# Sums of weights on VectorE, a quarter of the first modulations on VectorE with constant matmuls in TensorE's wait, positions added twice

## The chip, the cores and the metric

The kernel runs on one core of a Trainium2 chip. The core has a matrix engine (TensorE, PE in the profile; PEld is its weight load), a vector engine (VectorE, DVE), an activation engine (ScalarE, ACT), a general engine (GpSimd, POOL) and a queue from which nearly all DMA transfers are issued (SyncE, SP). Each engine executes its own instructions in order and waits on semaphores for the others. The metric is the time of one execution on the device, in microseconds (us).

## The reference

One layer over 1024 latent tokens with 256 context tokens in front, width 1024, all in float32:

```python
h = x + grid_pos_emb(rows)[None]                      # fixed sin/cos of row and column
mods   = split(silu(c) @ w_ada + b_ada, 9)            # shift, scale, gate of three sublayers
mods_c = split(silu(c_ctx) @ w_ada + b_ada, 9)        # the same for the context
def ffn_sublayer(h, shift, scale, gate, g, w_in, w_out):
    hn = modulate(rmsnorm(h, g), shift, scale)        # x * (1 + scale) + shift
    a, b = split(hn @ w_in, 2)                        # 1024 -> 2 x 2816
    return h + 0.5 * gate * ((silu(a) * b) @ w_out)
h  = ffn_sublayer(h,  ..., w_ffn1_in, w_ffn1_out);  hc = ffn_sublayer(hc, ...)
p_lat = project(h, ..., w_in); p_ctx = project(hc, ...)   # q, k, v, gates, o, u, vs, ga, gb
# mLSTM in both directions, the context gives its first state; spatial gating MLP;
# both projected by w_a, w_b, merged by sigmoid gates, projected by w_o
h = h + mods[5] * merge_branches(...)
h = ffn_sublayer(h, ..., w_ffn2_in, w_ffn2_out)
return rmsnorm(h, g_final)
```

## The kernel before, in words

Activations lie with the feature dimension on the partitions: `h[tb][d]` is a tile of 128 features by 512 tokens (`tb` 0 or 1, `d` 0 to 7). Every large product is made to float32's accuracy from two reduced-precision halves: `split` (L142 to 144) makes the high half by a copy on ScalarE (L143) and the low half by a subtraction on DVE (L144), and `mm3` issues three matmuls per term. So each weight tile passes through ScalarE and DVE before PE may use it, and DVE's `ring`, `wring` and `hl` subtractions are what most matmuls wait for if anything.

The stages in order of time: the start (0 to 51 us), the context's FFN input product (to 178), the latent FFN's input product, called the first gate stage here (178 to 602), its output product `w1o` (602 to 812), the context's output product and the projections, the mLSTM and the merge (812 to 2021), the second gate stage (2021 to 2451), the second output product with the final norm (2451 to the end).

**The start.** The first two modulations need `silu(c) @ w_ada`. Four quarters `qt` of 256 features each are loaded as eight pages (`ada_pages`, 256 KB a page); for each page PE does a matmul (`ada_mm`, tile `adr`, L811, executed in two passes); `ada_out` brings the row onto the partitions by small matmuls (tile `adc`, L820), adds the bias into `mods` (L824) and makes `smod` (L831). Meanwhile the context is normed (`nct`): squares on ScalarE, their sum `acc` on DVE (L196), a sum over partitions on PE (`p`), rstd on DVE in eleven small steps, a diagonal (`diag`, L210) that PE turns into a broadcast (`rb`, L214). `mod0(d)` then makes the context page `hnc[d]`: `nt` on DVE (L225), the high half on ScalarE, the low half on POOL for even `d` (L229), on DVE for odd `d` (L232). With `hnc` and split weights (`W.load`: tiles `raw` and `hl`) PE runs `proj` (`pa` and `pb`, L169). Ten matmuls on a constant (`junk`) fill PE before the first page.

**The gate stages.** Their class makes blocks of the product from seven smaller ones instead of eight, so sums and differences of weight blocks are needed: `presum` (L355, L356), the block of product 6 (L371) and of product 3 (L373), all on POOL (`G`), ahead of the split. A weight tile loaded for that is `rawq` (`rawh` for the first tiles of a stage). The class `Rows` does the like for the matrices of the mixing part (L1140 to L1146).

**w1o.** The class for it runs seven products in the order 1, 2, 4, 7, 6, 5, 3, of eleven steps each. A step loads a page of activations (`graw` or `gring`), for the first two products a weight page (`rw`), splits them and runs its matmuls. After product 2 the results are added to `h`, which `res` (L664) loads back from the spill buffer `hsp`; the start had stored h plus positions there.

**Order.** The program emits work in one order; a scheduler places each engine's instructions. `slow`, `later` and `todo` are queues of small functions; `pump` takes one from them as matmuls give credit (512 for three matmuls of 512 columns), and each function has a cost. So vector work is spread between matmuls at a rate that the costs set.

## Time and profile before

| | |
|---|---|
| median of 3 runs | 2685.7 us (2684.61 to 2685.88) |
| the profiled execution's own time | 2682.41 us |
| its span, first to last instruction | 2680.3 us |
| mean granted PE clock | 0.997 |
| PE busy | 2650.2 us (99%) |
| DVE busy | 1916.7 us (72%) |
| ACT busy | 1141.7 us (43%) |
| POOL busy | 440.6 us (16%) |
| DMA | 456.73 MB, mean 170 GB/s |

A row of the timeline or of a group names line, engine, operation and the tiles it writes and reads; a bracket at the end of a timeline row gives the idle time before it and whose end it waited for. Rows with an A.BC:D.EF stretch give each engine's busy time in that stretch, the granted clock (1.00 is full), the DMA share and GB/s. `x16` counts instructions as executed.

### The profile page before, as it was taken

What the parts mean: (1) busy time and instruction counts of PE and PEld (TensorE: products, weight loads), DVE (VectorE), ACT (ScalarE), POOL (GpSimd) and SP (SyncE); (2) the same over time, 40 slices, a digit from 0 to 9 for tenths busy, and PEclk for the clock granted to TensorE, in tenths of its full rate; (3) what the DMA queues carried; (4) which work ended last, traced back from release to release, by engine and by line L of the source; (5) the groups of instructions that cost most, each with busy time, mean ns of one, the idle gap of its engine ahead of it and who ended that gap; (6) DMA issues with size and microseconds to landing.
All of it is one profiled execution on the core that took longest, in us unless ns stands there. A gap on an engine that the chain in (4) does not pass through costs nothing.

```text
span 2680.3 us, 35678 instructions
## 1 busy us (share of the span) xinstructions
PE 2650.2 (99%) x12754; PEld 2210.3 (82%) x12754; DVE 1916.7 (72%) x3243; ACT 1141.7 (43%) x1952; POOL 440.6 (16%) x422
## 2 busy tenths in 40 slices
PE   9999999999999999999999999999999999999998
PEld 5998888888889878888888888888887788888887
DVE  4897688686979646687664868677568766675855
ACT  4664444344336525564443443121245444344432
POOL 0041333220000210000002005342102323230000
PEclk9999999999999999999999999999999999999999
DMA  8842344369578222356553467448140332337645
GB/s 299 315 173 99 142 165 149 114 217 327 156 254 281 85 79 86 106 169 199 194 176 105 140 238 268 166 167 279 58 159 24 126 140 99 135 122 274 201 157 173
DMA packets 202240, 456.73 MB, mean 170 GB/s; under 512 B 20432, under 2 KB 54480, under 8 KB 202064
## 3 DMA queue, kind: packets, MB, share of 16 engines
q1 hardware_dynamic: 202064, 454.47, 49.6%
q8 instruction: 100, 1.64, 0.3%
q14 instruction: 76, 0.62, 0.1%
HBM read 328.95 MB, written 125.51 MB: 170 GB/s over the span
## 4 chain that ended last, share of the span: by engine, by line
PE 89%; DVE 6%; issue 2%; DMA 1%; ACT 1%; SPq 0%; POOL 0%; POOLq 0%; ACTq 0%; DVEq 0%
PE pq L1240 17%; PE qa L389 17%; PE po L508 14%; PE qb L389 12%; PE pt L1719 9%; PE pr L1159 6%; PE pc L1030 2%; PE pn L1832 2%; PE pu L1559 2%; PE pa L169 1%; PE pb L169 1%; PE pkc L1219 1%; PE adr L811 1%; PE pn L1830 1%; DVE h L292 1%
## 5 line engine op out<-in xcount | busy, mean ns | idle before, releaser
L144 DVE TENSOR_TENSOR ring<-rawq,ring 128x512 fp32r<-128x512 f32 x408 | 310.6, 762 | 204.9 <-ACT ring L143 202.2
L508 PE MATMUL po<-gring,wring 128*128 128x512 f32 (+1 forms) x1896 | 425.1, 385 | 0.5 <-DMA gring<-fsp 0.5
L508 PEld LDWEIGHTS po<-gring,wring 128*128 128x128 f32 x1896 | 349.5, 188 | 71.9 <-issue 1.0
L143 ACT CAST ring<-rawq 128x512 fp32r<-128x512 f32 x408 | 252.9, 621 | 299.5 <-PE pq L1240 82.1
L389 PE MATMUL qa<-fc,ring 128*128 128x512 f32 x1056 | 252.6, 390 | 2.3 <-DVE ring L144 1.4
L389 PEld LDWEIGHTS qa<-fc,ring 128*128 128x128 f32 x1056 | 198.1, 188 | 44.2 <-DVE ring L144 1.8
L1240 PE MATMUL pq<-fc,ring 128*128 128x512 f32 x864 | 207.8, 393 | 0.0
L143 ACT CAST wring<-rw 128x512 fp32r<-128x512 f32 x154 | 95.9, 622 | 228.3 <-PE po L508 220.9
L1240 PEld LDWEIGHTS pq<-fc,ring 128*128 128x128 f32 x864 | 161.6, 188 | 33.3
L1719 PE MATMUL pt<-yp,ring 128*128 128x512 f32 x768 | 183.9, 396 | 1.2 <-ACT ug L1297 1.2
L144 DVE TENSOR_TENSOR wring<-rw,wring 128x512 fp32r<-128x512 f32 x154 | 106.3, 691 | 93.9 <-ACT wring L143 93.7
L1719 PEld LDWEIGHTS pt<-yp,ring 128*128 128x128 f32 x768 | 144.2, 188 | 30.7 <-ACT ug L1297 1.4
L1240 PE MATMUL pq<-fa,ring 128*128 128x512 f32 x576 | 142.3, 395 | 0.0
L1240 PE MATMUL pq<-fb,ring 128*128 128x512 f32 x576 | 138.2, 394 | 0.0
L389 PE MATMUL qa<-fb,ring 128*128 128x512 f32 x528 | 128.6, 394 | 3.7 <-ACT p L404 3.7
L389 PE MATMUL qa<-fa,ring 128*128 128x512 f32 x528 | 127.7, 391 | 1.2 <-DVE ring L144 0.7
L389 PE MATMUL qb<-fb,ring 128*128 128x512 f32 x528 | 126.8, 390 | 1.2 <-DVE p L406 0.6
L1240 PEld LDWEIGHTS pq<-fb,ring 128*128 128x128 f32 x576 | 107.7, 188 | 23.7 <-issue 0.2
L389 PE MATMUL qb<-fa,ring 128*128 128x512 f32 x528 | 126.2, 389 | 0.0
L389 PE MATMUL qb<-fc,ring 128*128 128x512 f32 x528 | 126.2, 389 | 0.0
L751 DVE SCALAR_TENSOR_TENSOR adacc<-adapg,sc,adacc 128x512 f32<-128x512 f32 x140 | 111.4, 814 | 20.1 <-DMA adapg<-in_w_ada_dram 19.3
L1240 PEld LDWEIGHTS pq<-fa,ring 128*128 128x128 f32 x576 | 106.9, 188 | 22.5 <-DVE ring L144 0.2
(342 smaller groups left out, 4803.9 us busy)
## 6 DMA issues: line engine op xcount, KB each, us to landing
adapg<-in_w_ada_dram SPq DMA_DIRECT2D x144, 256.0 KB, 3.7
fsp<-fhl SPq DMA_DIRECT2D x66, 512.0 KB, 2.6
gring<-fsp SPq DMA_DIRECT2D x66, 512.0 KB, 4.2
raw<-in_w1i_dram SPq DMA_DIRECT2D x44, 512.0 KB, 5.5
graw<-fsp SPq DMA_DIRECT2D x88, 256.0 KB, 3.6
rawq<-in_w1i_dram SPq DMA_DIRECT2D x38, 512.0 KB, 3.4
rawq<-in_w2i_dram SPq DMA_DIRECT2D x38, 512.0 KB, 3.6
fsp<-p SPq DMA_DIRECT2D x66, 256.0 KB, 2.1
```

What stands on the lines that cost most here:

```text
L143: S.copy(hl[:, 0, :], src)
L144: V.tensor_sub(hl[:, 1, :], src, hl[:, 0, :].bitcast(F32))
L169: T.matmul(pt, x, y, start=first and i == 0, stop=i == n - 1, skip_group_check=True)
L389: T.matmul(pt, hl[:, x, sl], pages[p][k][:, y, :], start=first and i == 0, stop=i == 11, skip_group_check=not first)
L508: T.matmul(pt[:, cs], w[:, x, sl], g[:, y, cs], start=grp and kp == 0 and i == 0, stop=kp == NFP - 1 and i == 2, skip_group_check=not grp)
L751: eng.scalar_tensor_tensor(acc, pgt, sc2[:, q, k:k + 1], acc, ALU.mult, ALU.add)
L1030: T.matmul(pt, hl[d // 4][:, x, sl], g[:, y, :], start=f == 0 and d % 2 == 0 and i == 0, stop=f == NF - 1 and i == 2, skip_group_check=True)
L1159: T.matmul(self.pt[m], pg[:, x, sl], hl[:, y, :], start=first and k == 0 and i == 0, stop=k == 3 and i == 2, skip_group_check=not first)
L1240: T.matmul(pt, hl[:, x, k * 128:(k + 1) * 128], pg[k][:, y, :], start=first and k == 0 and i == 0, stop=k == 3 and i == 2, skip_group_chec ...
L1559: T.matmul(pu[:, 0:257], ksl[:, kt * 128:(kt + 1) * 128], wv, start=True, stop=True)
L1719: T.matmul(pt, hl[:, x, k * 128:(k + 1) * 128], pg[:, y, :], start=kh + k + i == 0, stop=kh == 1 and k == 3 and i == 2)
L1832: T.matmul(pn[:, 0:257], qi[:, c_, :], self.C[d][:, c_, :], start=False, stop=c_ == 1)
```

## The change

1. At the start, quarter 3 is no longer multiplied on PE. Its pages are accumulated on DVE, page times `silu(c)` for the two conditions, then transposed and reduced, and summed over partition groups by one matmul per condition on the constant `grp4` (new function `ada_side`). The pages of quarter 1 and quarter 3 are loaded alternately, then quarter 2; seven more `junk` matmuls stand behind quarter 0; quarter 1's matmuls are cut in two around the sum of squares; the context pages are used in the order 0 to 3, 6, 7, 4, 5; `pos` and most constants are loaded later.
2. h plus positions isn't stored at the start. In w1o x is loaded again from the input during the second product, and the positions are added a second time (function `base`, tile `pos2`, 16 DVE additions).
3. The sums of weights of the gate stages and of the row matrices run on DVE instead of POOL; the sums of the first stage's first six tiles stay on POOL (`A.preload(G)`).
4. Small moves: the gap ahead of the context's second norm pages, two more empty steps before the second gate stage's broadcast, pages of `yp` and `raw` taken from the other half of a pool, x loaded one weight pair later.
5. At the end, the three last outputs that POOL makes are stored through ScalarE's DMA queue.

```diff
     def proj(pt, wl, pgs, first):
-        mm3(pt, [wk(wl, k) + (...) for k in range(NKT)], first)
+        mm3(pt, [wk(wl, k) + (...) for k in (0, 1, 2, 3, 6, 7, 4, 5)], first)
...
-        def presum(self, f):
+        def presum(self, f, eng=V):
...
-            G.tensor_tensor(s1, b1, b2, ALU.add)
-            G.tensor_tensor(b1, a1, b1, ALU.subtract)
+            eng.tensor_tensor(s1, b1, b2, ALU.add)
+            eng.tensor_tensor(b1, a1, b1, ALU.subtract)
...
                 if p == 6:
-                    G.tensor_tensor(a1, s["s1"], a1, ALU.subtract)
+                    V.tensor_tensor(a1, s["s1"], a1, ALU.subtract)
                 elif p == 3:
-                    G.tensor_tensor(a2, a2, a1, ALU.subtract)
+                    V.tensor_tensor(a2, a2, a1, ALU.subtract)
...
+                    if base is not None:
+                        for tb, d in [(0, d) for d in range(NKT)] + [(1, d) for d in range(NKT)]:
+                            load, add = base(hv, tb, d)
+                            later([load], 0)
+                            later([add], 1024)
                 elif p == 2:
...
-                    later([res(0, d) for d in range(4)], 512)
+                    if base is None:
+                        later([res(0, d) for d in range(4)], 512)
...
+    def ada_side(qt, accs):
+        bv = vs_("b_ada").rearrange("p (m d) -> p m d", m=9)
+        cs = slice(qt * QD, (qt + 1) * QD)
+        p8 = mm_ps("p8")
+        for q, acc in enumerate(accs):
+            red = cp.tile([128, 32], F32, name="adred", tag="adred", bufs=4)
+            ada_red(acc, red, 0)
+            T.matmul(p8[:, q * 16:q * 16 + 16], grp4, red[:, 0:16], start=True, stop=True)
+        for q in (1, 0):
+            for r in range(4):
+                sl = slice(32 * r, 32 * r + 32)
+                V.tensor_add(mods[sl, 0:2, q, cs], p8[...], bv[sl, 0:2, cs])
+            scale_mod(0, 1, q, "g_ffn1", cs)
...
-    for qt in (1, 2, 3):
-        apg.append(ada_pages(qt))
+    apg += ada_pages((1, 3))
+    nc.sync.dma_start(cst[:, 1], a["cst"][:, 128:256])
+    apg += ada_pages((2,))
...
+    sides = [t2("adacc") for _ in range(2)]
+    for k in range(NKT):
+        for q in range(2):
+            ada_acc(V, sides[q], ada_page(apg[2], k), q, k, k == 0)
+    for _ in range(7):
+        T.matmul(junk[:, 0:128], ones, ones, start=True, stop=True)
+    pr1 = ada_mm(apg[1], range(4))
     nct.rstd()
...
-                slow(nc.sync.dma_start, hsp[tb, f - 2], h[tb][f - 2], cost=0)
...
-            A.preload()
+            A.preload(G)
...
+    pos2 = A.rg.tile([128, 512], F32, name="ft", tag="ft", bufs=1)[:, 0:320]
+    nc.sync.dma_start(pos2, a["pos"])
+    def base(hv, tb, d):
+        return (lambda: nc.sync.dma_start(hv[tb][d], a["xT"][d, :, tb * 512:(tb + 1) * 512]),
+                lambda: add_pos(tb, d, hv, pos2))
...
             if p == 7:
-                G.tensor_tensor(b1, a1, b1, ALU.subtract)
+                V.tensor_tensor(b1, a1, b1, ALU.subtract)
...
-    nct.queue(smod[:, 1, 1, :], mods[:, 3, 1, :], hnc, gap=(1, 2, 12), cost=1280)
+    nct.queue(smod[:, 1, 1, :], mods[:, 3, 1, :], hnc, gap=(1, 2, 8), cost=1280)
...
-        dst[tb][k] = hnpage(k // 4, "yp")
+        dst[tb][k] = hnpage(1 - k // 4, "yp")
...
-    B.gate([n1_.rstd] + [nop] * 3 + [n1_.bcast] + ...)
+    B.gate([n1_.rstd] + [nop] * 5 + [n1_.bcast] + ...)
...
-        nc.sync.dma_start(out[d, :, ...], o_)
+        q = nc.scalar if pool_ and cs.stop == 512 else nc.sync
+        q.dma_start(out[d, :, ...], o_)
```

The order on PE at the very start, before and then with the change (`adr` are the pages' matmuls, eight to a quarter; `p` the sum of squares, later the group sums; `adc` the rows brought onto the partitions):

```order
L864 MATMUL junk<-ones 128x128 x10
L811 MATMUL adr<-adapg,sc_96 2x512 x16
L201 MATMUL p_237<-ones,acc 128x1 x2
L820 MATMUL adc<-cst,adrow 128x2 x4
L811 MATMUL adr<-adapg,sc_96 2x512 x8
L214 MATMUL rb<-diag,ones 128x256
L820 MATMUL adc<-cst,adrow 128x2 x4
L811 MATMUL adr<-adapg,sc_96 2x512 x8
L820 MATMUL adc<-cst,adrow 128x2 x4
L169 MATMUL pa<-hnc,hl 128x256 x12
```

```order
L893 MATMUL junk<-ones 128x128 x10
L824 MATMUL adr<-adapg,sc_96 2x512 x8
L914 MATMUL junk<-ones 128x128 x7
L824 MATMUL adr<-adapg,sc_96 2x512 x2
L201 MATMUL p_257<-ones,acc 128x1 x2
L824 MATMUL adr<-adapg,sc_96 2x512 x6
L833 MATMUL adc<-cst,adrow 128x2 x4
L214 MATMUL rb<-diag,ones 128x256
L833 MATMUL adc<-cst,adrow 128x2 x4
L824 MATMUL adr<-adapg,sc_96 2x512 x8
L849 MATMUL p_337<-adred,cst 128x16 x2
L169 MATMUL pa<-hnc,hl 128x256 x12
```

Eight page matmuls are gone, and the two on `adred` stand right ahead of the first `pa`. On DVE, the stretch that ends with the first weight splits of the context product, with the change:

```order
L225 SCALAR_TENSOR_TENSOR nt<-hc,smod,rb 128x256
L762 STREAM_TRANSPOSE adtr<-adacc 128x512 x2
L232 SCALAR_TENSOR_TENSOR hnc<-nt,mods,hnc 128x256
L763 TENSOR_REDUCE adred<-adtr 128x16 x2
L144 TENSOR_TENSOR hl<-raw,hl 128x1024 x3
L853 TENSOR_TENSOR mods<-p_337,vec 32x2x2 x5
L860 SCALAR_TENSOR_TENSOR smod<-mods,vec 128x2
L853 TENSOR_TENSOR mods<-p_337,vec 32x2x2 x3
L225 SCALAR_TENSOR_TENSOR nt<-hc,smod,rb 128x256
```

Before, two of these splits stood directly behind the same `hnc` step. The transposes and reductions now stand ahead of the three splits, and the additions of the side quarter behind them, ahead of the next `nt`.

In the second gate stage, on DVE, one round of weight splits, before and with the change (`ring` are splits, `p` and `u` the products' results, L355, L356 and L373 the sums of weights, which stood on POOL before):

```order
L417 TENSOR_TENSOR p_19966<-p_19966,qa 128x512
L144 TENSOR_TENSOR ring<-rawq,ring 128x512 x2
L420 TENSOR_TENSOR u_20029<-u_20029,qb 128x512
L144 TENSOR_TENSOR ring<-rawq,ring 128x512
L422 TENSOR_TENSOR u_20029<-u_20029,y_19989 128x512
```

```order
L417 TENSOR_TENSOR p_19714<-p_19714,qa 128x512
L144 TENSOR_TENSOR ring<-rawq,ring 128x512 x2
L373 TENSOR_TENSOR rawq<-rawq 128x512
L355 TENSOR_TENSOR s_19975<-rawq 128x512
L420 TENSOR_TENSOR u_19777<-u_19777,qb 128x512
L144 TENSOR_TENSOR ring<-rawq,ring 128x512
L356 TENSOR_TENSOR rawq<-rawq 128x512
L422 TENSOR_TENSOR u_19777<-u_19777,y_19737 128x512
```

Two sums now stand between the splits and the next product's addition (L420), a third behind the next split.

In w1o, on SP, the last loads of the second product, before and with the change (`h` before comes from the spill buffer, now from the input):

```order
L467 DMA rw<-in_w1o_dram 128x1024 x2
L477 DMA graw<-fsp_1978 128x512
L664 DMA h_5337<-hsp 128x512
L477 DMA graw<-fsp_1978 128x512
L664 DMA h_5338<-hsp 128x512
L664 DMA h_5339<-hsp 128x512
```

```order
L477 DMA graw<-fsp_1989 128x512
L467 DMA rw<-in_w1o_dram 128x1024
L1059 DMA h_5354<-in_xT_dram 128x512
L1059 DMA h_5355<-in_xT_dram 128x512
L477 DMA graw<-fsp_1989 128x512
L467 DMA rw<-in_w1o_dram 128x1024
L1059 DMA h_5356<-in_xT_dram 128x512
L1059 DMA h_5357<-in_xT_dram 128x512
```

All `rw` loads of this product stood ahead of the loads of `h`; now fourteen of the sixteen x loads stand ahead of the last `rw`.

More of the change, by code (lines that the diff above doesn't have):

```diff
@@ L121, in load @@
             else:
-                raw = hnp.tile([128, w], F32, name="raw", tag="pg1", bufs=8)
+                raw = hnp.tile([128, w], F32, name="raw", tag="pg0" if self.n == 2 else "pg1", bufs=8)
             self.n += 1
@@ L176, in proj @@
     def proj(pt, wl, pgs, first):
-        mm3(pt, [wk(wl, k) + (pgs[k][:, 0, :], pgs[k][:, 1, :]) for k in range(NKT)], first)
+        mm3(pt, [wk(wl, k) + (pgs[k][:, 0, :], pgs[k][:, 1, :]) for k in (0, 1, 2, 3, 6, 7, 4, 5)], first)
     def hnpage(tb, name):
@@ L796, in _build, with ada_pages, ada_page, ada_mm @@
     KP = 512 // QW
-    def ada_pages(qt):
-        pages = []
+    def ada_pages(qts):
+        res = [[] for _ in qts]
         for kp in range(NKT // KP):
-            pg = hnp.tile([128, KP, 2, QW], F32, name="adapg", tag=f"pg{1 - qt // 2}", bufs=8)
-            for i in range(KP):
-                src = a["w_ada"][kp * KP + i].rearrange("p (m c) -> p m c", m=9)[:, 0:2, qt * QW:(qt + 1) * QW]
-                nc.sync.dma_start(pg[:, i], src)
-            pages.append(pg)
-        return pages
-    def ada_mm(pages):
-        pr = sm_ps("adr")
-        for k in range(NKT):
-            T.matmul(pr[0:2, 0:2 * QW], sc2[:, :, k], pages[k // KP][:, k % KP].rearrange("p m c -> p (m c)"),
-                     start=k == 0, stop=k == NKT - 1)
+            for pages, qt in zip(res, qts):
+                pg = hnp.tile([128, KP, 2, QW], F32, name="adapg", tag=f"pg{1 - qt // 2}", bufs=8)
+                for i in range(KP):
+                    src = a["w_ada"][kp * KP + i].rearrange("p (m c) -> p m c", m=9)[:, 0:2, qt * QW:(qt + 1) * QW]
+                    nc.sync.dma_start(pg[:, i], src)
+                pages.append(pg)
+        return res
+    def ada_page(pages, k):
+        return pages[k // KP][:, k % KP].rearrange("p m c -> p (m c)")
+    def ada_mm(pages, ks, pr=None):
+        if pr is None:
+            pr = sm_ps("adr")
+        for k in ks:
+            T.matmul(pr[0:2, 0:2 * QW], sc2[:, :, k], ada_page(pages, k), start=k == 0, stop=k == NKT - 1,
+                     skip_group_check=True)
         return pr
@@ L1977, in _build @@
     n1_ = n3[1]
-    B.gate([n1_.rstd] + [nop] * 3 + [n1_.bcast] + B.F.late(fpage, lambda k: [lambda: n1_.inplace(k, m7, m6)]))
+    B.gate([n1_.rstd] + [nop] * 5 + [n1_.bcast] + B.F.late(fpage, lambda k: [lambda: n1_.inplace(k, m7, m6)]))
     def put(n_, tb, d, pool_, cs=slice(0, 512)):
@@ L1985, in put @@
             V.scalar_tensor_tensor(o_, o_, vc("g_final", d), n_.rb, ALU.mult, ALU.mult)
[L1986 removed]
+        q = nc.scalar if pool_ and cs.stop == 512 else nc.sync
+        q.dma_start(out[d, :, tb * 512 + cs.start:tb * 512 + cs.stop], o_)
     def bc(n_):
```

67 lines of the change are left out of this document (38 added, 29 removed).

## The prediction, on record before the result

> **What bounds the kernel now.** I read the page first, then busy time by stage, then what TensorE (PE) waits for. Columns of the second view: the stretch, its length, then each engine's busy time, the granted PE clock, the DMA share and GB/s.
>
> ```profile
> PE 2650.2 (99%) x12754; PEld 2210.3 (82%) x12754; DVE 1916.7 (72%) x3243; ACT 1141.7 (43%) x1952; POOL 440.6 (16%) x422
> ```
>
> ```profile
> 0.00:602.00 602.00, 592.19 (x3048) 490.83 (x3049) 457.05 (x667) 276.62 (x456) 142.17 (x98) 1.00 0.54 186
> 602.00:812.00 210.00, 209.50 (x930) 172.75 (x929) 169.43 (x292) 92.51 (x161) 0.00 (x0) 1.00 0.73 241
> 812.00:2021.00 1209.00, 1205.01 (x5894) 1014.69 (x5893) 834.98 (x1637) 496.11 (x850) 178.51 (x239) 1.00 0.48 164
> 2021.00:2451.00 430.00, 424.00 (x1859) 348.69 (x1858) 307.48 (x393) 189.42 (x329) 115.69 (x80) 1.00 0.34 120
> 2451.00:2680.30 229.30, 219.47 (x1031) 183.37 (x1029) 147.80 (x256) 87.08 (x157) 4.21 (x6) 0.98 0.58 195
> ...
> 178.00:602.00 424.00, 420.46 (x1854) 347.06 (x1853) 324.77 (x448) 178.76 (x310) 129.82 (x82) 1.00 0.41 144
> ```
>
> PE is the bound everywhere. It is not busy for 602.00 - 592.19 = 9.8 us before 602, 0.5 in w1o, 4.0 up to 2021, 6.0 in the second gate stage and 9.8 at the end: 30.1 in all, 3.5 of them in the first gate stage (178 to 602). A change can win here only by taking PE work away, or by ending some of these 30 us and the slow clock behind them.
>
> **The start.** PE, then VectorE (DVE):
>
> ```profile
> 0.97 4.63 PE L864 MATMUL junk<-ones 128*128 128x128 f32 x20 [0.97 <-POOL epst L86]
> ...
> 15.24 8.72 PE L811 MATMUL adr<-adapg,sc 128*2 128x512 f32 x16 [2.51 <-DMA adapg<-in_w_ada_dram]
> ...
> 33.98 7.03 PE L811 MATMUL adr<-adapg,sc 128*2 128x512 f32 x16
> ...
> 41.91 1.69 PE L169 MATMUL pa<-hnc,hl 128*128 128x256 f32 x12
> ...
> 50.91 0.28 PE L169 MATMUL pa<-hnc,hl 128*128 128x256 f32 x1
> ```
>
> ```profile
> 13.72 3.61 DVE L196 TENSOR_TENSOR acc<-acc,sq 128x256 f32<-128x256 f32 x7 [13.72 <-ACT sq L195]
> ...
> L751 DVE SCALAR_TENSOR_TENSOR adacc<-adapg,sc,adacc 128x512 f32<-128x512 f32 x26 | 18.8, 753 | 4.1 <-DMA adapg<-in_w_ada_dram 4.1
> ...
> L749 DVE TENSOR_SCALAR adacc<-adapg,sc 128x512 f32<-128x512 f32 x20 | 9.5, 482 | 0.0
> L755 DVE STREAM_TRANSPOSE adtr<-adacc 128x512 f32<-128x512 f32 x20 | 13.6, 698 | 0.0
> L756 DVE TENSOR_REDUCE adred<-adtr 128x16 f32<-128x512 f32 x20 | 13.5, 680 | 0.2
> L144 DVE TENSOR_TENSOR hl<-raw,hl 128x1024 fp32r<-128x1024 f32 x3 | 3.6, 1224 | 0.4 <-ACT hl L143 0.4
> ```
>
> (Rows 2 to 5 of that fence are groups: count | busy, mean ns.) PE loses the fourth quarter, the 7.03 us at 33.98. DVE gains 2 x 0.48 + 14 x 0.75 + 2 x 0.70 + 2 x 0.68 = 14.2 us by these means. Rows that follow one another overlap by some 0.08 us (the 3.61 us for seven sums of 425 ns in the start's groups is data-paced, so I take the overlap from the gate rows below: 0.69 long, 0.61 apart), which leaves about 12.9.
>
> Pages now land in the order quarter 1 and quarter 3 in turn, then quarter 2. A 256 KB page at the 348 GB/s of the clock row below takes 0.75 us; from 15.2 on, quarter 3's last page lands near 27, quarter 2's near 33, the first w1i tile near 34. DVE's chain is then: sums end 17.33; 16 accumulations 10.2, eleven small rstd steps 2.2 (0.2 each, estimated from 24.5 to 26.7 in the same trace), the diagonals 0.4: 30.3. Modulations and four `nt`/`hnc` steps, two transposes, two reductions: near 37. Three `hl` splits at 1.1: 38.1, 39.2, 40.3. PE can start `pa` at 38.1 in place of 41.91. It then waits, since the eight small additions of the side quarter (42.0), `nt` of 6 and 7 (43.0) and the rest stand behind the splits on DVE; `hnc` 6 is there at about 44.0, the last `hnc` at 46.2, the last matmul of the pair at 46.9 in place of 51.2. So PE's 7.03 us buys 4.3 at most, because DVE takes the bound. PE's wait of about 2 us at 42 is new, and such a wait has a price after it:
>
> ```profile
> 15.20:20.00 4.80, 4.76 (x8) 0.83 (x9) 1.72 (x5) 1.06 (x3) 0.00 (x0) 0.64 1.09 348
> ...
> 2093.70 4.61 PE L389 MATMUL qa<-fb,ring 128*128 128x512 f32 x12 [2.29 <-ACT p L404]
> ...
> 2094.00:2096.00 2.00, 2.00 (x7) 1.57 (x6) 2.00 (x5) 0.17 (x1) 0.00 (x0) 0.62 0.50 156
> 2096.00:2099.00 3.00, 3.00 (x10) 2.36 (x10) 2.35 (x4) 1.28 (x3) 1.17 (x1) 0.68 0.96 313
> ```
>
> After gaps of 2.51 and 2.29 us the granted clock fell to 0.64 and 0.62. If 2.0 us does that too, the 24 matmuls behind it, 0.13 each by the 1.54 us from `pa` to `pb`'s start (12 of them), take up to 1.9 us more. I take -3.3 for the start, the middle of -4.3 and -2.4 (bounds -4.5, and -0.5 if pages or splits come 2 us later still). The seven added junk matmuls, 14 passes of 0.23, take 3.2 us: the 2.51 of PE's wait cover most, and 0.7 delays quarter 1, whose pages now come 1.5 us apart where its passes need 0.9; so nothing.
>
> The Trainium skill, page "TensorE: Matmul & The Clock Gate", section "Part 1: The HAM clock gate", has the clock halve only after an idle window of about 3.4 us. By that rule the 2 us would cost nothing more and the start would give -4.3. The two gaps above, both shorter, speak against it.
>
> **Sums of weights from POOL to DVE.** POOL, then DVE beside it, then DVE's groups in the second gate stage:
>
> ```profile
> L355 POOL TENSOR_TENSOR s<-rawq 128x512 f32<-128x512 f32 x38 | 56.6, 1491 | 26.3 <-ACT ring L143 22.8 <-DMA rawq<-in_w1i_dram 2.4 <-DMA rawq<-in_w2i_dram 0.9
> ...
> 2061.21 3.44 POOL L356 TENSOR_TENSOR rawq<-rawq 128x512 f32<-128x512 f32 x2
> ```
>
> ```profile
> 2061.72 3.47 DVE L144 TENSOR_TENSOR fc<-h,fc 128x512 fp32r<-128x512 f32 x2
> 2065.11 1.28 DVE L292 TENSOR_TENSOR h<-h 128x512 f32<-128x512 f32 x2
> ...
> L144 DVE TENSOR_TENSOR ring<-rawq,ring 128x512 fp32r<-128x512 f32 x114 | 94.9, 834 | 76.4 <-ACT ring L143 74.8
> L422 DVE TENSOR_TENSOR u<-u,y 128x512 f32<-128x512 f32 x21 | 31.8, 1512 | 0.1
> L144 DVE TENSOR_TENSOR ring<-s,ring 128x512 fp32r<-128x512 f32 x19 | 19.9, 1048 | 0.2
> L144 DVE TENSOR_TENSOR fhl<-p,fhl 128x512 fp32r<-128x512 f32 x10 | 15.6, 1558 | 0.0
> ```
>
> Two subtractions beside POOL take 3.47 us; two others right behind, 1.28. So undisturbed, one is 0.69 long and they stand 0.61 apart. Against 0.69 the four groups are inflated by 16 + 17 + 7 + 9 = 49 us; the stage's 80 POOL instructions cost DVE 80 x 0.61 = 49 when they move. DVE's total stays as it was, with 122 us of the 430 free; what goes is the clumping: a needed split no longer stands 1.1 us behind a sum that is needed later. The same holds in the first gate stage with its 82 POOL instructions, and for the 32 of the row matrices. PE's gaps that this bears on are the 2.29 above and these:
>
> ```profile
> PE qa L389 <- ACT p L404: 3.7, 2, 2.3
> PE rb L214 <- DVE diag L210: 2.9, 2, 1.8
> ...
> PE qa L389 <- DVE ring L144: 2.1, 2, 1.4
> ...
> PE pvc L1318 <- DVE nt L225: 0.8, 1, 0.8
> ```
>
> ```profile
> 1936.82 3.92 PE L1719 MATMUL pt<-mx,ring 128*128 128x512 f32 x16 [0.89 <-DVE mx L144]
> ```
>
> In the second gate stage 6.0 us of gaps and about 1.7 of slow clock (5 us at 0.62 to 0.68) are at stake; half goes, -4.0. Before it, the 0.78 at `pvc` (its norm is now emitted earlier) and part of the 0.89 (the heads' sums no longer beside `mx`): -1.5 of 4.0. In the first gate stage -0.5 of 3.5. The two more empty steps ahead of the broadcast let PE do other matmuls where it waited 1.1 for `diag`; that is in the -4.0. The swapped pages of `yp` and `raw` change addresses alone: 0, since the loads that need them are asked for long before PE's use. Together -6.0; bounds -11, if nearly all of it goes, and +3, if DVE's order brings new gaps. ScalarE's copy that ended the 2.29 is late because casts ahead of it on its queue wait for POOL and DVE; both waits shorten, neither vanishes.
>
> The Trainium skill, page "SBUF — State Buffer", section "SBUF: two separate sides", has the loser of the port shared by DVE and GpSimd block for the other's whole instruction. If each of the 194 moved ones had blocked DVE for 1.1 us, moving would free 213 us for 118 and nearly all gaps would go. The inflation of 49 for 80 instructions is a little over half of that, so I don't take it.
>
> **Positions added twice.** At the start sixteen 256 KB stores go, and x comes one weight pair later:
>
> ```profile
> 50.00:100.00 50.00, 48.93 (x407) 48.52 (x405) 39.57 (x52) 30.15 (x41) 0.00 (x0) 1.00 0.85 292
> ```
>
> Only 1.07 us are to be had; less traffic and the later x pull in opposite directions: 0, bounds -1 and +2. In w1o sixteen DVE additions and the loads of x, which replace loads of the same bytes, come into the second product, 632 to 662:
>
> ```profile
> 625.00:660.00 35.00, 35.00 (x157) 28.93 (x155) 19.51 (x35) 16.35 (x30) 0.00 (x0) 1.00 0.96 331
> ...
> 638.29 1.02 SPq L467 DMA_DIRECT2D rw<-in_w1o_dram  x2
> ```
>
> DVE is idle for 15.5 of these 35 us; the additions take 16 x 0.61 = 9.8. But SP now puts two x loads between one w1o tile and the next, from about 624 on (where the ring slot for the fourth step's input comes free, then one each 2.7 us). A round is 256 + 512 + 2 x 256 KB, 4.0 us at 331 GB/s, against 2.7 us that PE takes for a step (209.5 us busy for 7 products of 11 steps). Seven rounds bring the product's last w1o tile at about 653; before, it was asked for at 638.3. PE needs its split at 659.7, some 3 us after the earliest, and DVE must still make the next product's first combinations before 662.4, where about 1 us is left. I take +0.5, bounds 0 and +8.
>
> **The end.**
>
> ```profile
> 2673.45 2.05 DVE L1985 SCALAR_TENSOR_TENSOR h<-h,vec,rb 128x256 f32<-128x256 f32 x5 [1.77 <-ACT rbs L1991]
> ...
> 2674.24 3.77 SPq L1986 DMA_DIRECT2D out_dram<-h  x8
> ```
>
> Eight issues take SP 3.77 us. With five on SP and three on ScalarE's queue the last starts some 1.4 us earlier. The trace has no issue from ScalarE; if it takes twice SP's 0.47 the gain stays, if ScalarE's three wait for its copy and POOL it is lost: between +0.5 and -1.9, I take -1.3, nearer to SP's own rate.
>
> **The sum.** -3.3 - 6.0 + 0 + 0.5 - 1.3 = -10.1, from the profiled execution's 2682.4 (span 2680.3) to 2672.3. The runs' median, 2685.7, lies 3.3 above it: 2675.6.
>
> **Rivals.** A, only start and end count: gaps in the gate stages come back elsewhere, as DVE works off the same total in order. For it: 49 against 49. Against: the gaps stand where POOL and DVE ran together. -4.1, thus 2681.6. B, DVE's queue blocks in the gate stages: a sum that waits for its weight tile now stands ahead of splits that PE needs, where POOL waited alone. A gap like the one at 2093.7 costs 2.3 and 1.7 of slow clock, 4.0; slower by over 0.2% from the third such gap on, and with three 2693.6. Against: POOL's sums waited for these tiles 2.4 + 0.9 us in all. C, the second product of w1o stalls: each late round adds up to 1.3 us once the 1 us is used up; five with a slow clock behind are +8, thus 2683.1. D, all goes: the start's wait leaves the clock at 1.00, and the gaps of the middle end but for a few: -4.3 - 11 - 1.3 = -16.6, thus 2669.1. For its first part stands the 1.4 us gap behind `ring` in the first gate stage, whose mean clock is 1.00; the 2.29 stands against it. (The clock rule of the Trainium skill named above would make D's first part sure.)
>
> **Chances.** Forecast 0.48, A 0.22, B 0.10, C 0.08, D 0.12. A measurement of this kernel can tell 0.2%, 5.4 us, from no change. Faster (under 2680.3): the forecast, D and a little of A, 0.67; same, most of A, C and some of B: 0.24; slower, the rest of B: 0.09. The range runs from D's 2669 to past A and C, 2684.
>
> **What would show it.** Quarter 3's passes gone from PE, first `pa` near 38, DVE without idle from 17 to 46, a PE gap near 42 with a clock under 1 behind it. In the gate stages DVE's `ring<-rawq` mean near 690 ns, the 2.29 us gap under 1 us, the clock at 1.00 in 2020 to 2120. PE busy throughout 632 to 665. The end: last landing 1.3 us sooner after `rbs`. It is wrong if PE's idle time in the two gate stages isn't below 9.5 us, or if gaps stand behind `wring` near 660.

## The result, and the profile after

The changed kernel takes 2664.92 us (median of 4 runs, 2663.7 to 2665.11) against 2685.79 (4 runs, 2684.61 to 2686.82): 0.9921 of before, 95% interval 0.9904 to 0.9939. It is faster by some 21 us, twice the forecast and below the range. A second measurement of the same kernel gave 0.9936 (0.9924 to 0.9949), some 17 us. The profiled execution fell from 2682.4 to 2663.7, its span from 2680.3 to 2661.8: 18.4 us, which the stages below divide among them.

The page of the changed kernel, and its busy time by stage (columns as in the prediction; the stages' bounds have moved with the kernel):

```profile
PE 2642.0 (99%) x12748; PEld 2209.4 (83%) x12748; DVE 1939.8 (73%) x3487; ACT 1144.1 (43%) x1951; POOL 138.3 (5%) x220
```

```profile
0.00:594.20 594.20, 587.98 (x3045) 492.32 (x3046) 474.66 (x775) 277.93 (x455) 13.57 (x16) 0.99 0.52 181
594.20:804.80 210.60, 209.53 (x928) 172.39 (x927) 180.03 (x309) 94.07 (x162) 0.00 (x0) 1.00 0.72 241
804.80:2013.00 1208.20, 1205.02 (x5895) 1014.20 (x5894) 843.91 (x1676) 495.77 (x849) 120.55 (x198) 1.00 0.48 164
2013.00:2434.20 421.20, 421.20 (x1860) 348.04 (x1859) 293.44 (x472) 189.37 (x329) 0.00 (x0) 1.00 0.34 122
2434.20:2661.80 227.60, 218.25 (x1027) 182.48 (x1025) 147.71 (x256) 86.97 (x157) 4.21 (x6) 0.99 0.58 198
```

PE's time without work fell from 30.1 to 19.8 us, and its busy time by 8.2, part of it a clock that no longer falls. The fourth row is the striking one: in the second gate stage PE is busy for 421.20 of 421.20 us, where it had missed 6.0. Where the time went is read from the first matmul of each stage in the two traces (leads and gains are taken before rounding):

| stage begins at | before | after | lead | gained in the stage ahead |
|---|---|---|---|---|
| first gate stage | 178.9 | 174.3 | 4.6 | 4.6 (start and context product) |
| w1o | 602.6 | 594.2 | 8.4 | 3.8 (first gate stage) |
| context's output product | 815.8 | 808.4 | 7.5 | -0.9 (w1o) |
| second gate stage | 2021.6 | 2013.2 | 8.4 | 0.9 (projections, mLSTM and merge) |
| second output product | 2451.8 | 2434.2 | 17.5 | 9.2 (second gate stage) |
| end | 2680.3 | 2661.8 | 18.4 | 0.9 (end) |

The two gate stages make 13.0 of the 18.4. These are the changed kernel's groups on DVE in the second one (count | busy, mean ns | idle before them):

```profile
L144 DVE TENSOR_TENSOR ring<-rawq,ring 128x512 fp32r<-128x512 f32 x114 | 78.6, 690 | 94.9 <-ACT ring L143 94.7
L417 DVE TENSOR_TENSOR p<-p,qa 128x512 f32<-128x512 f32 x22 | 15.1, 687 | 17.3 <-PE qa L389 17.3
...
L422 DVE TENSOR_TENSOR u<-u,y 128x512 f32<-128x512 f32 x21 | 14.4, 685 | 0.0
...
L355 DVE TENSOR_TENSOR s<-rawq 128x512 f32<-128x512 f32 x19 | 13.0, 685 | 0.3 <-DMA rawq<-in_w2i_dram 0.3
```

The weight splits fell from 834 to 690 ns, L422 from 1512 to 685, and a moved sum (L355) costs 685 on DVE where POOL took 1491. DVE makes 79 instructions more in this stage and is busy for 14 us less (307.5 to 293.4).

The first 80 us of that stage hold all its gaps. Before, in two halves, then the changed kernel from the same place in its program:

```profile
2021.30:2060.00 38.70, 36.41 (x158) 28.50 (x158) 35.21 (x58) 26.56 (x47) 7.37 (x6) 1.00 0.02 7
2060.00:2100.00 40.00, 36.29 (x152) 29.17 (x151) 37.18 (x51) 19.38 (x35) 11.74 (x8) 0.96 0.22 76
```

```profile
2013.00:2051.70 38.70, 38.70 (x173) 31.31 (x172) 35.62 (x64) 28.58 (x51) 0.00 (x0) 1.00 0.02 7
2051.70:2091.70 40.00, 40.00 (x178) 33.13 (x177) 38.31 (x64) 20.85 (x37) 0.00 (x0) 1.00 0.27 100
```

DVE is the engine without reserve here, 72.4 of 78.7 us busy before and 73.9 after. But before it got 58 + 51 = 109 instructions done in that time, now 128, of which 14 are sums that POOL made before.

### The profile page after: what moved, and what is told of

Read it like the earlier page. It is cut to its first block, busy times and chain, and to the rows that moved or that the text cites. A ratio compares the mean times of both kernels' runs of the same rounds, so it can differ in the third digit from the quotient of the medians.

```text
span 2661.8 us, 35493 instructions
## 1 busy us (share of the span) xinstructions
PE 2642.0 (99%) x12748; PEld 2209.4 (83%) x12748; DVE 1939.8 (73%) x3487; ACT 1144.1 (43%) x1951; POOL 138.3 (5%) x220
## 4 chain that ended last, share of the span: by engine, by line
PE 90%; DMA 4%; DVE 3%; issue 2%; ACT 1%; SPq 0%; POOL 0%; POOLq 0%; ACTq 0%; DVEq 0%
PE qa L389 18%; PE pq L1290 17%; PE qb L389 13%; PE po L508 12%; PE pt L1769 9%; PE pr L1209 5%; PE pa L169 2%; PE pb L169 2%; PE pc L1080 2%; PE pn L1882 2%; PE pu L1609 2%; DMA rw<-in_w1o_dram 1%; PE pkc L1269 1%; PE pvc L1368 1%; PE pn L1880 1%
## 5 line engine op out<-in xcount | busy, mean ns | idle before, releaser
L144 DVE TENSOR_TENSOR ring<-rawq,ring 128x512 fp32r<-128x512 f32 x408 | 281.2, 690 | 223.1 <-ACT ring L143 222.1
L1290 PE MATMUL pq<-fa,ring 128*128 128x512 f32 x576 | 142.3, 395 | 0.0
```

The source lines that it names most:

```text
L144: V.tensor_sub(hl[:, 1, :], src, hl[:, 0, :].bitcast(F32))
L1290: T.matmul(pt, hl[:, x, k * 128:(k + 1) * 128], pg[k][:, y, :], start=first and k == 0 and i == 0, stop=k == 3 and i == 2, skip_group_chec ...
```

## The experiments

The theories from the two traces: **one**, moving the sums ended PE's gaps in both gate stages, for POOL's work beside DVE slowed DVE (1a) or for the longer chain over two engines (1b); **two**, what the start gains depends on the stores that are gone; **three**, short waits at the start bring PE's clock down. Ratios are to the kernel before on the same chip, with 95% intervals; times are medians. Traces are one execution each.

**All sums back on POOL** (the rest as changed).

```diff
-        def presum(self, f, eng=V):
+        def presum(self, f, eng=G):
-                    V.tensor_tensor(a1, s["s1"], a1, ALU.subtract)
+                    G.tensor_tensor(a1, s["s1"], a1, ALU.subtract)
...
-                V.tensor_tensor(b1, a1, b1, ALU.subtract)
+                G.tensor_tensor(b1, a1, b1, ALU.subtract)
```

> The changed kernel with all sums of weights back on POOL, everything else as changed. Theory 1 (moving the sums ended PE's gaps in both gate stages, 3.8 + 9.2 us of the gain): about 13 us slower than the changed kernel, 2677 to 2679; the 2 us gap with its slow clock is back near the second gate stage's start, and DVE's mean on the weight splits is back near 830 ns there. Rival (the small moves, two more empty steps and the other gap, did it in the second gate stage): 4 to 5 us slower at most, 2668 to 2670, and the second gate stage has no gap over 1 us.

Measured: 2684.44 against 2683.32, ratio 1.0005 (0.9996 to 1.0015). More was lost than either theory said: without the sums, all the rest together is worth nothing that a median shows. Its waits of PE in the second gate stage (us in total, times, longest):

```profile
PE qa L389 <- ACT p L404: 3.1, 1, 3.1
PE rb L214 <- DVE diag L210: 1.1, 1, 1.1
PE qb L389 <- ACT fb L143: 0.8, 1, 0.8
```

The gap that had been 2.29 is back as 3.1, and the wait for the diagonal is back although the two empty steps are there. Both gate stages take as long as before (423.6 and 430.2 us). The lead of the rest is lost in between: this execution is 4.9 us ahead of the kernel before at the first gate stage and at w1o, and 4.8 behind it at the second gate stage. Part of that stands beside POOL's sums for the row matrices: PE waits 0.72 and 2.40 us for the splits of `mx` near 1935 and 1938, with a granted clock of 0.50 from 1938 to 1944, where the kernel before has the one wait of 0.89.

**Only the sums on DVE** (the kernel before otherwise; the reverse of the edit above, with the first stage's head on POOL).

```diff
-        def presum(self, f):
+        def presum(self, f, eng=V):
...
-            A.preload()
+            A.preload(G)
```

> The kernel before with only the sums of weights moved to DVE. Theory 1: 13 us faster than before, 2672 to 2674, with both gate stages free of gaps over 1 us apart from the wait for the diagonal (1.1 us). Rival (small moves): 3 to 5 us faster, 2681 to 2683. Second rival (the lead that the start gives let the gate stages run without gaps): under 5 us faster, since start and small moves are as before.

Measured: 2668.99, ratio 0.9946 (0.9929 to 0.9963), 14.3 us faster. Its second gate stage, from the same place:

```profile
2023.00:2444.00 421.00, 421.00 (x1860) 348.25 (x1859) 293.68 (x473) 189.62 (x329) 0.00 (x0) 1.00 0.33 122
```

No gap, no wait for the diagonal, the same 421 us, with the old start, the old number of empty steps and a lead of 0.2 us at the first gate stage. Theory one holds for the place; both rivals fall. By stage it gains 2.9 us in the first gate stage and 9.4 in the second.

**POOL work that nobody needs** (the changed kernel; the sums stay on DVE).

```diff
             eng.tensor_tensor(b1, a1, b1, ALU.subtract)
+            self.idle(s1, b1, 3)
+
+        def idle(self, x, y, n=1):
+            if self.name == "w2i":
+                for _ in range(n):
+                    G.tensor_tensor(cst[:, 2:5], *(v[:, 0:384].rearrange("p (a b) -> p a b", b=128) for v in (x, y)), ALU.subtract)
...
                     V.tensor_tensor(a1, s["s1"], a1, ALU.subtract)
+                    self.idle(s["s1"], a1)
...
                     V.tensor_tensor(a2, a2, a1, ALU.subtract)
+                    self.idle(a2, a1)
```

> The changed kernel with extra POOL instructions in the second gate stage, five subtractions of 384 columns a weight pair, whose results nobody reads; DVE still makes all sums, in the same order. Theory 1a (POOL's reads beside DVE's two-input instructions slow DVE, whoever needs the result): DVE's mean on the weight splits rises from 690 to over 800 ns in that stage and part of the gaps come back, 3 to 9 us, 2668 to 2674. Theory 1b (the longer chain over POOL, DVE to POOL to ScalarE to DVE, made the gaps, not the slowing): no gap comes back, 2665 within 1 us, whatever the mean.

Measured: 2674.00, ratio 0.9966 (0.9953 to 0.9979), 9 us slower than the changed kernel, at the upper end of 1a; the second gate stage is 9.6 us longer than there. Its second gate stage: the stage, two of its groups on POOL and DVE, and PE's first gap:

```profile
2014.00:2445.00 431.00, 426.05 (x1861) 348.49 (x1861) 356.03 (x473) 188.09 (x329) 132.97 (x99) 1.00 0.34 119
```

```profile
L362 POOL TENSOR_TENSOR cst<-s,rawq 128x384 f32<-128x384 f32 x76 | 102.9, 1355 | 213.7 <-DVE rawq L356 170.9 <-issue 34.1 <-POOL cst L362 5.5
...
L144 DVE TENSOR_TENSOR ring<-rawq,ring 128x512 fp32r<-128x512 f32 x114 | 97.6, 864 | 27.2 <-ACT ring L143 27.0
...
L425 DVE TENSOR_TENSOR p<-p,qa 128x512 f32<-128x512 f32 x22 | 15.0, 682 | 2.6 <-PE qa L397 2.6
...
2082.27 2.15 PE L397 MATMUL qa<-fb,ring 128*128 128x512 f32 x7 [2.19 <-ACT p L412]
```

Ninety-nine instructions without a reader raise DVE's busy time from 293.4 to 356.0, 0.63 us each, and the old 2.2 us gap stands at its old place, though no result of POOL is read and DVE is never idle in the 15 us ahead. So slowing DVE is enough to make such a gap. It strikes selectively: the splits, which read two tiles of SBUF, rise to 864 ns, while L425, which reads one of its operands from PSUM, stays at 682. In the kernel before it is the same: L417 took 687 beside splits of 834. This is what the Trainium skill states (page "SBUF — State Buffer", section "SBUF: two separate sides"): DVE instructions with two SBUF inputs and GpSimd instructions exclude one another. Its "whole instruction" is an upper bound here: on average 0.63 us of DVE's time is lost for 1.34 of POOL's.

The load is heavier than in the kernel before, though. DVE makes the sums as well, and ahead of the gap POOL runs seven instructions in a row, where before it ran three in 4.9 us. And in the kernel before ScalarE itself waited for a sum of POOL shortly ahead of the gap. The kernel before, then this run:

```profile
2082.54 1.78 DVE L144 TENSOR_TENSOR ring<-rawq,ring 128x512 fp32r<-128x512 f32 x1
2086.04 1.77 DVE L422 TENSOR_TENSOR u<-u,y 128x512 f32<-128x512 f32 x1
2087.30 1.14 ACT L143 CAST ring<-rawq 128x512 fp32r<-128x512 f32 x2 [1.72 <-POOL rawq L373]
```

```profile
2071.68 11.17 POOL L362 TENSOR_TENSOR cst<-s,rawq 128x384 f32<-128x384 f32 x7 [6.92 <-issue]
2076.16 2.96 DVE L144 TENSOR_TENSOR ring<-s,ring 128x512 fp32r<-128x512 f32 x2
```

One thing more differs: weight loads are asked for later (one at 2084.7, in the changed kernel at 2077.1; whether through DVE's slower splits or POOL's late readings isn't shown), and DVE's sum (L355) waits 32.3 us for them in 16 waits, 0.3 in the changed kernel. This run's two other gaps over 1 us, 1.08 at 2118 and 1.02 at 2139, stand behind such waits of 2.29 and 3.96. So 1a is shown to be enough for the first gap, under a heavier load; how the 9.6 us of this run and the gaps of the kernel before divide among the causes is not shown. In the kernel before, all of them end when the sums leave POOL.

**Only the start** (the kernel before with the new order of the start, h plus positions stored).

```diff
+    apg += ada_pages((1, 3))
...
+    ada_side(3, sides)
...
                 slow(n1[tb].sq, f - 2)
                 slow(nc.sync.dma_start, hsp[tb, f - 2], h[tb][f - 2], cost=0)
```

> The kernel before with only the start as changed (a quarter on DVE, seven constant matmuls, order of loads, x one weight pair later), h plus positions stored as before. If the start is worth what the trace shows up to the first gate stage, 4.6 us faster, 2681 to 2682. If part of the 4.6 comes from the stores that are gone between 50 and 178 us: 2.5 to 3 us faster, 2683. The gate stages keep their gaps in both cases.

Measured: 2685.29 against 2683.32, ratio 1.0009 (0.9999 to 1.0018). The start alone gives nothing. Its first `pa` stood at 37.0 (41.9 before), but the first gate stage began at 179.8, later than before:

```profile
89.20 4.39 PE L169 MATMUL pa<-hnc,hl 128*128 128x256 f32 x22 [1.87 <-DVE hl L144]
102.48 2.73 PE L169 MATMUL pb<-hnc,hl 128*128 128x256 f32 x14 [1.11 <-DVE hl L144]
...
ACT hl L143 <- DMA raw<-in_w1i_dram: 10.5, 6, 3.2
```

The last row is a wait of ScalarE between 46 and 180 us: the copies of the weight splits wait 10.5 us for the weights' DMA. The kernel before has it too, 9.5 us in five waits, but there PE's gaps between 50 and 178 us come to 1.7, against 3.9 here. In the changed kernel this wait does not appear at all in that stretch. (The window of PE's rows ends at 105 us, inside the second one.) The load of `pos2`, which nothing reads here, stays in this edit and in the next.

**Positions stored** (the changed kernel with the stores at the start and the loads of them in w1o).

```diff
                 slow(n1[tb].sq, f - 2)
+                slow(nc.sync.dma_start, hsp[tb, f - 2], h[tb][f - 2], cost=0)
...
-           lambda tb, d, t: nc.sync.dma_start(hsp[tb, d], t), tick, base=base)
+           lambda tb, d, t: nc.sync.dma_start(hsp[tb, d], t), tick)
```

> The changed kernel with h plus positions stored at the start and loaded back in w1o, as before; the rest as changed. Theory 2 (with the start shortened, the stores make the weight splits of the context product late, and what the start gained is given back between 50 and 178 us): gaps behind the weight splits at about 89, 102 and 159 us of 1 to 2 us each with a lower clock behind, and the first gate stage begins 5 to 6 us later than in the changed kernel; w1o gives 1 us back; in all 4 to 5.5 us slower, 2669 to 2670.5. Rival (the late splits came from POOL's sums of the first tiles or from x coming one weight pair later): no such gaps, within 1 us of 2665.

Measured: 2668.95, ratio 0.9943 (0.9926 to 0.9959), at the lower edge of what was expected, though the median alone doesn't tell it from the changed kernel's. The trace does (the last PE row is cut off by its window):

```profile
88.61 0.50 PE L169 MATMUL pa<-hnc,hl 128*128 128x256 f32 x2 [0.74 <-ACT hl L143]
89.97 4.31 PE L169 MATMUL pa<-hnc,hl 128*128 128x256 f32 x22 [0.86 <-DVE hl L144]
103.26 2.10 PE L169 MATMUL pb<-hnc,hl 128*128 128x256 f32 x13 [1.11 <-DVE hl L144]
...
ACT hl L143 <- DMA raw<-in_w1i_dram: 9.7, 6, 4.4
```

The first gate stage begins at 180.6, 6.3 us later than in the changed kernel. So theory two holds. Whether the stores delay the loads by their place in SP's order or by the rate that they take isn't separated by these runs.

**The start as before** (the kernel before with the sums on DVE and the positions added twice; the edits of parts 2 and 3 of the change).

> The kernel before with the sums on DVE and the positions added twice; start, small moves and end as before. If the start is worth 4.6 us only where the stores are gone: 5 to 7 us slower than the changed kernel (start 4.6, end 1, small moves 1), 2670 to 2672, no gap over 0.5 us between 60 and 178. If the missing stores alone make the 4.6: 2666 to 2668.

Measured: 2669.41, ratio 0.9943 (0.9928 to 0.9958), 0.6 us under the first expectation and well above the second. PE has no gap over 0.5 us between 60 and 176. Its first gate stage begins at 176.2. With it the four combinations stand side by side; the figure is the lead over the kernel before at the first gate stage, one profiled execution each:

| | h plus positions stored | positions added twice |
|---|---|---|
| start as before | 0 (before), 0.2 (only sums) | 2.7 |
| new start | -0.9 (only start), -1.7 (positions stored) | 4.6 (changed; 4.0 to 6.0 in eight others of that kind) |

Of the 2.7, 1.8 stand already at the first `pa` (40.1 in place of 41.9), before the first store at 43.0. In this execution quarter 1 ran at the full clock, behind a wait as long as the one before:

```profile
15.16 7.03 PE L818 MATMUL adr<-adapg,sc 128*2 128x512 f32 x16 [2.61 <-DMA adapg<-in_w_ada_dram]
```

The stretch from the first `pa` to the first gate stage, which that clock doesn't touch, takes 137.0 us before, 136.1 here, 142.8 and 142.3 with the new start and the stores, and 134.8 to 137.3 with the new start and without them. So the two parts have no worth that adds up: the new start loses 1 to 2 us with the stores, and without them gains some 3.7 (an estimate: 4.6 less the 0.9 that the missing stores give); the missing stores give 0.9 with the old start and 5.5 to 6.3 with the new one.

**Without the small moves** (gap of the second context norm, empty steps, pages of `yp`).

```diff
-    nct.queue(..., gap=(1, 2, 8), cost=1280)
+    nct.queue(..., gap=(1, 2, 12), cost=1280)
...
-        dst[tb][k] = hnpage(1 - k // 4, "yp")
+        dst[tb][k] = hnpage(k // 4, "yp")
...
-    B.gate([n1_.rstd] + [nop] * 5 + [n1_.bcast] + ...)
+    B.gate([n1_.rstd] + [nop] * 3 + [n1_.bcast] + ...)
```

> The changed kernel with the small moves undone (gap of the context's second norm, empty steps before the second gate stage's broadcast, pages of yp). Theory 1 (the sums alone end the gaps): the wait for the diagonal (0.4 to 1.1 us) and the one at pvc (0.8) come back, nothing else: 1 to 2 us slower than the changed kernel, 2666 to 2667. Rival (the small moves matter for the second gate stage, where the changed kernel has not one gap): 4 us or more slower, 2669 and above.

Measured: 2664.24, ratio 0.9924 (0.9909 to 0.9939): the changed kernel's time. Neither the wait for the diagonal nor the one at `pvc` came back; both go with the sums on DVE, as in the run with only these.

**Constant matmuls between quarter 1's pairs.**

```diff
-    pr1 = ada_mm(apg[1], range(4))
+    pr1 = ada_mm(apg[1], range(2))
+    fill(4)
...
```

> The changed kernel with 16 more matmuls on the constant between quarter 1's pairs of passes, where PE waits for pages. Theory 3 (the waits of 1.1 us between the pairs, each under the 2.3 us seen before, together bring the clock down to 0.5 from 31 to 35 us): the clock stays at 1.00 there, quarter 2's passes take 7.0 in place of 8.7 us, the first pa comes near 37.3, the first gate stage begins 1 to 2 us sooner; 2663 to 2664. Rival (DVE's chain sets the start's end anyway): the clock stays up, but the first gate stage begins within 0.5 us of the changed kernel's 174.3.

Measured: 2665.47, ratio 0.9930 (0.9915 to 0.9945). The waits between the pairs are filled, and quarter 2 takes 8.72 us all the same. So those waits are not what slows it: theory three falls in this form. The wait right ahead of quarter 2 stays, at 0.64 us.

**Constant matmuls before quarter 2**, and **no added constant matmuls** (the seven of the change left out).

```diff
     nct.bcast()
+    def fill(n):
+        for _ in range(n):
+            T.matmul(junk[:, 0:128], ones, nct.diag[:, 0:128], start=True, stop=True)
+
+    fill(4)
...
     ada_out(1, pr1)
+    fill(5)
```

> The changed kernel with nine more constant matmuls right behind the broadcast, ahead of quarter 2, where PE has only tiny matmuls and a wait for 3.7 us. Theory 3b (the clock falls on what the array does, not on how long PE's row is empty: the tiny matmuls count as idle): the granted clock stays at 1.00 from 30 to 36 us, quarter 2's passes take 7.0 us in place of 8.7, the first pa comes 0.5 to 1.5 us sooner; within 1.5 us of the changed kernel in all. Rival (something else lowers the clock there, such as the passes themselves): 8.7 us again.

```diff
-    for _ in range(7):
-        T.matmul(junk[:, 0:128], ones, ones, start=True, stop=True)
```

> The changed kernel without the seven added constant matmuls behind quarter 0. By the prediction's step (they lie in a wait, worth nothing): the same time within 0.5 us, though the first pairs of quarter 1 run at half clock. Rival: the slower pairs make the sum of squares and so the whole chain on DVE later, 1 to 2 us at the first gate stage.

Beside both stood the changed kernel once more:

> The changed kernel itself, to stand beside the three runs of this group on the same chip: 0.9921 of before within 0.001, 2663 to 2667.

Measured: 2665.69, ratio 0.9930 (0.9918 to 0.9942); 2666.94, 0.9936 (0.9922 to 0.9950); and 2668.38, 0.9936. The three can't be told apart. Quarter 2 in the two edits, in that order:

```profile
30.48 7.03 PE L824 MATMUL adr<-adapg,sc 128*2 128x512 f32 x16
```

```profile
29.31 7.03 PE L824 MATMUL adr<-adapg,sc 128*2 128x512 f32 x16 [1.09 <-issue]
```

The first is what theory 3b said, but it is one execution. The second ran at full clock as well: with the same tiny matmuls and the same wait ahead as in the changed kernel, and without the constant matmuls. Over the eleven profiled executions with the new start, ten have that stretch unfilled; seven of these ran quarter 2 slowly (8.4 to 8.7 us), three in 7.03. So the same stretch goes both ways, and one execution with it filled doesn't settle 3b. What decides stays open. The Trainium skill (page "TensorE: Matmul & The Clock Gate", section "Part 1: The HAM clock gate") speaks of a window of about 3.4 us that runs freely and isn't set by the kernel's start; the stretch is 3.7 us long (26.04 to 29.76 in the changed kernel), but no run here shows the window itself, or that the tiny matmuls count as idle in it. Nor does it matter for the end: the four-way table's last cell holds variants of both kinds. The first gate stage began at 174.6 with the stretch filled and at 173.4 in the changed kernel beside it.

The seven constant matmuls of the change are worth nothing that shows: without them quarter 1's pairs took 1.88 us as with them, not at half clock as was expected, and the first gate stage began at 172.9.

**The end on one queue.**

```diff
-        q = nc.scalar if pool_ and cs.stop == 512 else nc.sync
-        q.dma_start(out[d, :, ...], o_)
+        nc.sync.dma_start(out[d, :, ...], o_)
```

> The changed kernel with all last outputs issued by SP again. If the issues set the end (the prediction's step): 1.3 us longer from the last broadcast to the end, and as much slower. If the rate of the transfers sets it (1.05 MB at 280 to 340 GB/s is 3.1 to 3.8 us, about what SP's eight issues took): 0.4 to 0.7 us longer, no difference that a median shows.

Measured: 2667.86, ratio 0.9937 (0.9925 to 0.9948), beside 0.9936 of the changed kernel measured with it. In the traces the last broadcast to the end takes 8.5 us (2656.28 to 2664.8) against 7.6 (2654.23 to 2661.8): 0.9 us, between the two expectations, and nothing that the median shows. The issues of the changed kernel's end:

```profile
2655.94 2.30 SPq L2037 DMA_DIRECT2D out_dram<-h  x5
2656.23 1.71 ACTq L2037 DMA_DIRECT2D out_dram<-h  x3
```

Issuing ends 1.5 us sooner than with SP's eight in 3.77 (same time here); the rest is lost behind it: SP's stores then take 2.4 us to land in place of 1.8, with the rate at some 335 GB/s.

## Why the prediction was wrong

**The start (-3.3).** Right as far as the step goes: `pa` began at 38.9 (38.1 forecast), with a slower clock in it, though at another place: quarter 2 ran slowly, from 29.76 on, before any wait at 42.

```profile
29.76 8.72 PE L824 MATMUL adr<-adapg,sc 128*2 128x512 f32 x16 [1.06 <-issue]
...
32.00:34.00 2.00, 2.00 (x4) 0.37 (x3) 2.00 (x6) 1.10 (x4) 1.42 (x2) 0.50 1.04 409
```

`pa` follows PE's passes and two small matmuls without a gap, here and in every trace with the new start, so PE and not DVE sets its beginning. The 2 us wait on `hnc` was two of 0.3 to 0.4; the clock fell behind these as well, to 0.50 between 46 and 48. Where quarter 2 ran at full speed (only the start), `pa` began at 37.0 and the wait came, 1.75 us at 42.9, with the clock at 1.00 behind it. Taken with the stores, the stretch to the first gate stage gave 4.6, inside the bounds of both steps together. By the four-way table the start gives about 3.7 of that, near the forecast, but with the stores it gives less than nothing, which the step did not foresee.

**Positions at the start (0, bounds -1 and +2).** Wrong as a step of its own. "Only 1.07 us are to be had" counted PE's gaps of the kernel before, up to 100 us (1.7 up to 178). With the shorter start those gaps grow to 3.9 and 4.1 if the stores stay, with a slower clock behind: without the new start the missing stores are worth about 0.9 us, with it 5.5 to 6.3.

**Sums (-6.0).** This is the step that failed. The mechanism was right, its effect was sized too small: "half goes" was to give -4.0 in the second gate stage and -0.5 in the first, and the runs show 9.2 and 3.8 there, with no gap of the old ones left in either; 13.0 in place of 4.5. Alone the sums give 14.3 by the median, beyond the bound of -11. The -1.5 forecast between the stages can't be checked: 0.9 was measured, but that stretch takes 1203.6 to 1214.4 us in the fourteen traces.

The reason given for half was partly wrong: "DVE's total stays as it was". The inflation, put at 49 us for four groups, is 62 over all of DVE (307.5 + 79 x 0.61 - 293.4), and the moved sums cost 48, so DVE gains 14. That alone doesn't explain why everything went. In the first 80 us, where the gaps stand, DVE makes 19 instructions more than before, but 14 of them are the sums; the five others, at 0.61 an estimated 3 us, are less than the 6.0 us of gaps. So the clumping that the prediction named, a needed instruction behind a slow one, cost more than half of the gaps; how much of it was DVE slowed and how much ScalarE waiting for POOL's sum stays open. Rival A, with 49 against 49 for it, and B fall with it; D, with "a few" gaps left, was the nearest and still too small. (The 1.4 us gap behind `ring` that D puts in the first gate stage lies in the second, at 2067; the first has one of 1.40 behind `p`. Both left the clock at 1.00, so its argument stands.) The rule of the Trainium skill on the shared port, which the prediction quoted (page "SBUF — State Buffer", section "SBUF: two separate sides") and didn't take, came out nearer: by it "nearly all gaps would go", and they went, though at a lower price than a whole instruction each.

**w1o (+0.5).** Measured 0.9, and not by the mechanism named, so its nearness is luck:

```profile
625.00:660.00 35.00, 34.93 (x155) 28.56 (x154) 27.66 (x44) 15.44 (x27) 0.00 (x0) 1.00 0.86 316
...
617.30:652.30 35.00, 35.00 (x156) 28.93 (x155) 25.63 (x47) 16.38 (x29) 0.00 (x0) 1.00 0.98 364
```

In the changed kernel PE misses 0.07 us of the 35 there; DMA ran at 364 GB/s while x was loaded (331 was reckoned with), so the last w1o tile was asked for at 642.7, and the additions lay in DVE's idle time. The 0.9 comes from a wait of 1.0 near 799, in the last product. Such a wait varies from 0.3 to 1.3 between executions, and the run with only the sums on DVE, which loads `h` back as before, has one of 1.01.

**The end (-1.3).** 0.9 by the trace.

## What to carry to other kernels

When VectorE has no reserve in a stretch, look at what GpSimd does beside it: here a GpSimd subtraction that reads SBUF took on average about half its own length out of VectorE's two-input instructions, needed or not: 62 us for sums that VectorE makes itself in 48. So a helper engine can cost more than it carries. Judge such a move over the stretch where the waiting stands, not over the stage's sum. And weigh changes that touch the same queue together: a shorter start was worth nothing as long as sixteen stores went out among the loads that it needed sooner.

## What the hardware showed that was not expected

- Ninety-nine GpSimd subtractions without a reader took 62.6 us from VectorE. VectorE's additions and subtractions of 128x512 with an operand in PSUM had means of 676 to 687 ns in every kernel, beside GpSimd or not.
- The same stretch of tiny matmuls (sixteen in 2.1 us, the broadcast, and a wait of 1.1 us: 3.7 us in all) was followed by half the clock in seven executions of ten and by the full clock in three. TensorE counts as busy in it for 2.7 of 3.7 us.
- The length of a gap doesn't tell whether the clock falls. With the positions stored, two gaps of 0.74 and 0.86 us within 2.1 us were followed by a granted clock of 0.50 from 92 to 94 us; in the kernel before, gaps of 1.40 and 1.42 us left it at 1.00. One and the same start had a gap of 2.51 us with a clock of 0.64 behind it (before) and one of 2.61 with the full clock (the start as before). So the slow clock that the prediction put behind a wait of 2 us, up to 1.9 us, comes in some executions only.
- Medians of one and the same changed kernel were 0.9921 and 0.9936 of before on two occasions. Waits of 0.5 to 2.6 us behind ScalarE at about 1590 and VectorE at about 1810 come and go between executions. Effects under 3 us were read from the traces here, not from medians, and those are one execution each: the lead at the first gate stage alone spreads over 2 us.
